# Seven modulation blocks of layer 0: from the tensor engine's products to sums on three other engines

## The chip, the core and the metric

The kernel runs on one core of a Trainium2 chip. The metric is the device time of one execution in microseconds (us), as the median of several runs. The engines are called as the profile calls them: PE (TensorE matmul), PEld (its weight load), DVE (VectorE), ACT (ScalarE), POOL (GpSimd) and SP (SyncE, whose queue issues the DMA transfers). Each engine takes its instructions strictly in the order in which they stand in its queue; an instruction whose inputs are not there holds up everything behind it.

## What is computed

The reference is a stack of three transformer layers on 512 tokens of width 1024, with 256 context tokens. What matters here is the start of layer 0, where every gain and shift comes from two condition vectors (the latent `c` and the context's `c_ctx`) by one product with a 1024 x 6144 matrix:

```python
silu_c, silu_cc = jax.nn.silu(c), jax.nn.silu(c_ctx)
mod_lat = (silu_c @ w_ada[i] + b_ada[i])[:, None, :]
mod_ctx = silu_cc @ w_ada[i] + b_ada[i]
sh_a, sc_a, g_a, sh_m, sc_m, g_m = jnp.split(mod_lat, 6, axis=-1)      # the same split of mod_ctx
h_lat, h_ctx = x * (1.0 + sc_a) + sh_a, xc * (1.0 + csc_a) + csh_a
y_lat, y_ctx = gqa_mixer(h_lat, h_ctx, w_qkv, q_norm, k_norm, w_o, ...)  # q, k, v = h @ w_qkv; norm; rope; attention
x = layer_norm(alpha * x + g_a * y_lat, ...)                            # then the MLP with sh_m, sc_m, g_m
```

Only `sh_a` and `sc_a` are needed before the projections to q, k and v. The gate `g_a` and the three vectors of the MLP are needed after the attention.

## The kernel before

All activations are kept transposed and split into a high and a low part, so that a float32 product is three products in the fast type (`mm3`, lines 137 to 141: one record each on L139, L140 and L141).

The 6144 columns of the modulation are made in 12 blocks of 512 columns. A block is a Python generator whose steps are issued between pieces of other work (`Flow`, lines 61 to 95: every chain that is open takes one step after each piece). For each block two transfers of 1 MB bring 512 rows each of the block's columns into tiles called `adaw`, three of which exist in this stage (`ada_bufs = 3`, line 418). `ada_steps` (line 199) then makes both conditions' products on PE: eight matmuls in four column groups of the array (L217), a copy of the four partial sums to the single tile `row512` by ACT (L221), four transposes of it on PE (L225), and on DVE one sum over the groups (L227) and the addition of the bias (L229), into the tile `MOD0`.

`ada_pooled` (line 231) makes the same vectors another way. In layer 1 it is used for 12 blocks, the first four of them for both conditions, and in the last layer for 12 blocks with one condition. Its steps, with `both=True`:

- two transfers to two `adaw` tiles (L239);
- eight DVE instructions that multiply the eight tiles of rows by the second condition's numbers and add them up into `row512` (L246 once, then L248 seven times, each reading what the one before wrote), and eight ACT instructions that multiply the same tiles by the first condition's numbers in place (L251), each after the DVE instruction that reads the same tile;
- three POOL additions that fold the eight tiles into one, of 2048, 1024 and 512 columns (L255);
- per condition four transposes on PE (L260), then on DVE the sum over partitions (L262) and the bias (L263).

The stage that the change concerns is `gqa` (line 409), from its line 492 to line 519. It holds the projections: for the column blocks `blk` 2 (keys and values), 0 and 1 (queries), and for the six token tiles, `products` issues 24 matmuls per piece and half, the results go from PSUM to `qn`, `kn` and `V` by ACT and DVE, and key chains (`key_steps`) and rope chains (`q_rope`) run beside them. At every second token tile one of the seven open modulation blocks (4, 5, 8, 9, 6, 7, 10) is added to the flow:

```python
if t % 2 and ada:
    flow.add(ada.pop(0))
```

`flow.finish()` (line 518) issues what is left of all chains before the attention's first step, the transposes of queries on L695. A scheduler orders each engine's queue afterwards by priorities and dependencies, so that what the code issues late can stand somewhat earlier. Block 11 is made in the attention, and blocks 0 to 3 before the projections; these five stay as they are.

Of the kernel before, what the change touches and what calls it, by code (L numbers as in the profile page):

```python
# [16 lines left out]
PSUM = bass.MemoryType.PSUM  # L17
# [6 lines left out]
LAG = 4  # L24


class Bump:
    """tiles laid out by hand in given regions of a bigger tile (views [128, n], in its type)"""
# [32 lines left out]
class Flow:  # L61
    """chains of steps that are issued beside the tensor engine's main work"""
# [16 lines left out]
    def finish(self, gen=None):  # L79
        """until the chain (all of them) has ended, beside work that was laid by; the other chains go half as fast"""  # L80
        n = 0
        while gen in self.gens if gen is not None else self.gens:
            if self.fill:
                self.fill.pop(0)()
            n += 1
            self.step([gen] if gen is not None and n % 2 else None)
# [10 lines left out]
class Base:  # L97
# [45 lines left out]
    def rsqrt(self, out, ms, n, scale):  # L143
        """out = (ms * scale + eps) ** -0.5 on [128, n]; ms is overwritten"""
        nc = self.nc
        nc.vector.tensor_scalar(out=ms, in0=ms, scalar1=scale, scalar2=EPS, op0=ALU.mult, op1=ALU.add)
        nc.gpsimd.tensor_tensor(out=out, in0=ms, in1=self.mhalf[:, :n], op=ALU.pow)

# [1 line left out]
    def setup(self):  # L150
        nc, cp, i = self.nc, self.cp, self.i
# [5 lines left out]
        # the activations' split transposes, time-shared by all phases  # L157
# [5 lines left out]
    def load_cols(self, groups, ps, pool, tag, keep=None):  # L163
        """rows of vectors [n, 128] -> one tile of columns; groups: list of (name, ap [n,128])"""
# [34 lines left out]
    def ada_steps(self, a, b, pool, ps, bias, beside=False, spare=False):  # L199
        """512 columns of the modulation vectors: silu(c) @ w (both conditions at once),  # L200
        four row groups of the array at a time, then summed and turned to one column per 128;
        beside: beside an attention's start, in its tiles and those of the weights; spare: the second half in one of these"""
# [28 lines left out]
    def ada_pooled(self, a, b, pool, ps, bias, both=False):  # L231
        """the same beside a phase that leaves the other engines idle: they weigh and sum the rows of a partition (DVE
        for the second condition, if both are asked for); then the sums are turned, and the partitions summed"""
# [19 lines left out]
        x, y = ts  # L253
# [14 lines left out]
    def gains(self, name, sc, sh, g=None, b=None):  # L268
        """columns G, B with h = xhat * G + B for h = (xhat * g + b) * (1 + sc) + sh"""
# [28 lines left out]
    def tok(self, j, k, t):  # L298
        """part j of the split transposed activations: rows of tile k, token tile t (4, 5: the context)"""
# [3 lines left out]
class GqaNet(Base):  # L303
# [1 line left out]
    def gqa_tables(self, kv, pool):  # L305
        """rope tables with the gains of q (and its 1/8) and k folded in: [128, token tile, 64]"""
# [19 lines left out]
    def head_rs(self, pool, x, n, out):  # L326
        """out [128, n] = rsqrt(mean of squares) of the heads of 64 of x [128, n*64]"""
# [14 lines left out]
    def rope64(self, pool, x, n, w, t):  # L342
        """the rope of x [128, n*64], with gains, in place; the context has gains only"""
# [22 lines left out]
    def modulated(self, pool, ps, x, T, gain, c, u):  # L366
        """T's columns from c: the split transpose of a token tile's rows x, times and plus the gain's columns; half u of
        the channels"""
# [18 lines left out]
    def key_steps(self, pool, ps, kn, K, t):  # L387
        """the keys of a token tile: normed, turned by their positions, transposed twice, split"""
# [18 lines left out]
    def gqa(self):  # L407
        nc, i, tc, flow = self.nc, self.i, self.tc, self.flow
        W = i["gqa_w_qkv"][0]
        with ExitStack() as ph:  # L410
# [6 lines left out]
            with tc.tile_pool(name="q0", bufs=1, reuse_waits="tile") as pool, tc.tile_pool(name="q0ps", bufs=2, reuse_waits="tile", space=PSUM) as ps:  # L417
# [8 lines left out]
                def load(t, u):  # L426
                    # the rows wait where the queries come
# [13 lines left out]
                def gains(u):  # L441
                    """columns G, B of half u of the channels, for both conditions"""
# [50 lines left out]
                ada = [self.ada_steps(0, b, pool, ps, None) for b in (4, 5, 8, 9, 6, 7, 10)]  # L493
# [60 lines left out]
    def out_weights(self, W, u):  # L554
        """256 columns of an output projection's weights, split: steps"""
# [10 lines left out]
    def attend(self, units, pool, pss, psp, stages):  # L566
        """softmax attention in units of 128 queries of one head (two, where there are few keys); the scores
        of a unit run LAG units ahead of the transposes of its weights, and their products with v follow
        by the group of four.  stages: unit -> other work beside it, as (PE, then Activation, then DVE) parts"""
# [7 lines left out]
        with self.tc.manual_schedule():  # L577
            for n in range(N + LAG + 6):
# [12 lines left out]
                if n < N:  # L591
# [5 lines left out]
                    if n == 0:  # L597
                        # brings the table of the exponential beside the first maximum
# [41 lines left out]
    def turn(self, pool, psp, g, xs):  # L640
        """the transposed weights of a unit into the group's [128 keys, key tile, head % 2, head // 2, 128]"""
# [19 lines left out]
class GqaGroup:  # L661
    """128 queries of the four heads that share a key head"""
# [11 lines left out]
    def bias(self, xs, m):  # L674
        """minus the scaled maximum"""
# [62 lines left out]
class Seg:  # L738
    """tokens: the split transposed activations T, the sum R [128, 8, n] (first read from S), the gate's columns g"""
# [5 lines left out]
class MlpNet(GqaNet):  # L745
    def stats(self, halves):
        """mean and rsqrt(var + eps) of rows given as PSUM halves [128, 512]: columns 2 and 3 are the factor and the offset"""
# [11 lines left out]
    def rows_of(self, ps, R, c):  # L759
        """the 128 tokens at column c of R as rows, in two halves"""  # L760
# [8 lines left out]
    def along(self, ps, cols):  # L769
        """[128, k, 256]: the columns (k for each of two token tiles) along every row"""  # L770
# [7 lines left out]
    def norm_steps(self, pool, ps, R, c0, res, hs):  # L778
        """layer norm of 256 tokens at column c0 of R [128, 8, n], then per column tile
        R = xhat * res[0] + res[1] (if res) and the split of xhat * G + B (hs: G, B, hi, lo)"""  # L780
# [32 lines left out]
    def w_out(self, W, ps, segs, after):  # L813
        """R = S + g * (T^T W)^T, the product's columns on partitions; the last four column tiles go by groups of
        256 tokens, each followed by the steps after(its number)"""
# [27 lines left out]
    def mlp(self, i, ps, segs, extra, ready, after, zp, gp):  # L843
        """R += g * (relu(h w1)^2 w2)^T in chunks of 256 hidden columns; the first two and the last two chunks go by
        groups of 256 tokens: ready: the steps that a group waits for, after: as in w_out; zp, gp: room"""
# [38 lines left out]
        def one(x, s, c):  # L884
            # a tile's weights are split a piece ahead
# [25 lines left out]
    def cols1(self, pool, ps):  # L911
        """the vectors of block 1 as columns"""
# [9 lines left out]
    def ln_cols(self, i, w, scale):  # L922
        """the gain and bias columns of norm w of layer i times scale"""
# [57 lines left out]
class MlaHead:  # L981
    """the 512 queries of one head; unit x is token tile x"""
    last = 3
# [49 lines left out]
    def low(self):  # L1033
        # a copy of the high part beside the sum where the partitions differ
# [10 lines left out]
class MlaNet(MlpNet):  # L1045
    def mla(self):
# [3 lines left out]
        with ExitStack() as ph:  # L1050
# [6 lines left out]
            # rows of keys and queries by the parity of the head: its 64 plain dims lie at 64 * parity,  # L1057
            # its 32 rotated ones beside them, and the rest are zero
# [18 lines left out]
    def turned_steps(self, pool, ps, xs, gain, hi, lo):  # L1077
        """two token tiles of rows xs, normed, times the gain, into the split columns hi, lo [128, k, 256]"""
# [19 lines left out]
    def mla_in(self, pool, m, spare):  # L1098
        """spare: room for the low part of the query weights, until the keys come"""
# [47 lines left out]
        # the weights of the rotated dims of all heads' queries  # L1147
# [7 lines left out]
        # the rotated dims of the keys  # L1155
# [44 lines left out]
    def turn32(self, out, x, at):  # L1200
        """out (32 rows from row at) = x [128, 32] transposed, as a product with the identity"""
        self.nc.tensor.matmul(out, lhsT=x, rhs=self.ident, start=True, stop=True, tile_position=(0, at))

    def rope32(self, x, tmp, base):
        """x [128, 4, 32] rotated in place"""
# [149 lines left out]
class PreNet(MlaNet):  # L1355
    def row_bcast(self, ps, pool, cols, name, out):
        """out [128, 1024] = the vector in columns [128, 8] along every row"""
# [1337 lines left out]
```

## Time and profile before

| what | value |
|---|---|
| median of 3 runs | 2687.36 us (2686.46 to 2691.48) |
| span of the profiled execution | 2685.0 us |
| PE busy | 2584.2 us, 96% of the span, 14954 instructions |
| DVE, ACT, POOL busy | 1789.9, 1154.3 and 611.1 us (67%, 43%, 23%) |
| chain that ended last | PE 30%, ACT 1%, DVE 1% of the span |

The page is read from the span downwards: PE is busy in nearly all of it, and the chain that ended last is mostly PE. The share of another engine is an average over very different stages, so the prediction goes to the stage itself, the stretch from about 62 to 158 us.

### The profile page before, as it was taken

What the parts mean: (1) busy time and instruction counts of PE and PEld (TensorE: products, weight loads), DVE (VectorE), ACT (ScalarE), POOL (GpSimd) and SP (SyncE); (2) the same over time, 40 slices, a digit from 0 to 9 for tenths busy, and PEclk for the clock granted to TensorE, in tenths of its full rate; (3) what the DMA queues carried; (4) which work ended last, traced back from release to release, by engine and by line L of the source; (5) the groups of instructions that cost most, each with busy time, mean ns of one, the idle gap of its engine ahead of it and who ended that gap; (6) DMA issues with size and microseconds to landing.
All of it is one profiled execution on the core that took longest, in us unless ns stands there. A gap on an engine that the chain in (4) does not pass through costs nothing. (4 is left out here: it accounts for less than half of the span.)

```text
span 2685.0 us, 37836 instructions
## 1 busy us (share of the span) xinstructions
PE 2584.2 (96%) x14954; PEld 2112.6 (79%) x14954; DVE 1789.9 (67%) x3102; ACT 1154.3 (43%) x2016; POOL 611.1 (23%) x445
## 2 busy tenths in 40 slices
PE   8999999999999999999999899989999999999998
PEld 5666689888888898777787678877678888888887
DVE  4558847887777577788489998576675533534445
ACT  4357835333333235655364344253563223532222
POOL 0224322232222013333133234043140011000000
PEclk9999999999999999999999999999999999999999
DMA  8600221333333112010155454233122233222221
GB/s 313 210 32 1 64 95 34 124 128 124 125 111 102 62 38 69 19 33 17 64 167 173 137 176 157 95 110 115 49 66 100 87 94 139 73 94 94 95 94 63
DMA packets 178643, 264.82 MB, mean 99 GB/s; under 512 B 18019, under 2 KB 116954, under 8 KB 177954
## 3 DMA queue, kind: packets, MB, share of 16 engines
q1 hardware_dynamic: 173010, 257.89, 29.2%
q10 hardware_dynamic: 5456, 4.51, 0.6%
q8 instruction: 118, 1.93, 0.3%
q14 instruction: 59, 0.48, 0.1%
HBM read 256.81 MB, written 5.58 MB: 98 GB/s over the span
## 5 line engine op out<-in xcount | busy, mean ns | idle before, releaser
L129 DVE TENSOR_TENSOR wl<-raw,wh 128x1024 fp32r<-128x1024 f32 (+1 forms) x301 | 442.6, 1483 | 305.7 <-ACT wh L126 303.6
L126 ACT CAST wh<-raw 128x1024 fp32r<-128x1024 f32 (+1 forms) x301 | 306.9, 1035 | 611.8 <-PE mm L140 443.7
L139 PE MATMUL mm<-TL,wh 128*128 128x512 f32 (+2 forms) x1512 | 563.2, 374 | 6.0 <-ACT TL L384 4.5
L140 PE MATMUL mm<-TL,wh 128*128 128x512 f32 (+2 forms) x1512 | 558.8, 370 | 4.0 <-DVE TL L385 3.9
L141 PE MATMUL mm<-TL,wl 128*128 128x512 f32 (+2 forms) x1512 | 557.5, 369 | 0.0
L139 PEld LDWEIGHTS mm<-TL,wh 128*128 128x128 f32 (+1 forms) x1512 | 285.1, 189 | 60.2 <-ACT TL L384 5.4
L140 PEld LDWEIGHTS mm<-TL,wh 128*128 128x128 f32 (+1 forms) x1512 | 285.7, 189 | 54.2 <-DVE TL L385 5.6
L141 PEld LDWEIGHTS mm<-TL,wl 128*128 128x128 f32 (+1 forms) x1512 | 285.3, 189 | 52.3
L139 PE MATMUL mm<-TC,wh 128*128 128x256 f32 (+1 forms) x672 | 224.3, 334 | 12.6 <-ACT low L864 12.5
L637 POOL TENSOR_SCALAR p<-p,sm 128x768 f32<-128x768 f32 (+1 forms) x160 | 156.2, 979 | 296.1 <-DVE sm L634 195.3
L141 PE MATMUL mm<-TC,wl 128*128 128x256 f32 (+1 forms) x672 | 223.4, 333 | 0.0
L140 PE MATMUL mm<-TC,wh 128*128 128x256 f32 (+1 forms) x672 | 223.4, 333 | 0.0
L255 POOL TENSOR_TENSOR XN<-XN 128x2048 f32<-128x2048 f32 (+2 forms) x36 | 117.9, 3275 | 297.1 <-ACT XN L251 278.5
L139 PE MATMUL mm<-gh,wh 128*128 128x256 f32 (+1 forms) x544 | 179.6, 330 | 0.0
L140 PE MATMUL mm<-gl,wh 128*128 128x256 f32 (+1 forms) x544 | 178.6, 328 | 0.0
L141 PE MATMUL mm<-gh,wl 128*128 128x256 f32 (+1 forms) x544 | 178.0, 328 | 0.0
L255 POOL TENSOR_TENSOR low<-low 128x2048 f32<-128x2048 f32 (+2 forms) x36 | 111.5, 3097 | 178.4 <-ACT low L251 176.5
L139 PEld LDWEIGHTS mm<-TC,wh 128*128 128x128 f32 x672 | 127.5, 190 | 28.1 <-ACT low L864 13.8
L600 DVE TENSOR_REDUCE sm<-s 128x1 f32<-128x768 f32 (+1 forms) x144 | 132.6, 921 | 22.5 <-PE s L1010 11.4
L140 PEld LDWEIGHTS mm<-TC,wh 128*128 128x128 f32 x672 | 127.8, 190 | 14.1
L141 PEld LDWEIGHTS mm<-TC,wl 128*128 128x128 f32 x672 | 127.7, 190 | 13.1
L657 PE MATMUL pt<-ident,p 128*128 128x128 f32 x768 | 116.1, 281 | 17.7 <-ACT pT L658 7.8
(614 smaller groups left out, 4981.9 us busy)
## 6 DMA issues: line engine op xcount, KB each, us to landing
raw<-in_mlp_w_dram SPq DMA_DIRECT2D x64, 1024.0 KB
raw<-in_w_in_dram SPq DMA_DIRECT2D x26, 1024.0 KB
XN<-in_w_ada_dram SPq DMA_DIRECT2D x24, 1024.0 KB
low<-in_ada_w_dram SPq DMA_DIRECT2D x24, 1024.0 KB
raw<-in_ffn_w_in_dram SPq DMA_DIRECT2D x22, 1024.0 KB
adaw<-in_w_ada_dram SPq DMA_DIRECT2D x21, 1024.0 KB
raw<-in_ffn_w_out_dram SPq DMA_DIRECT2D x11, 1024.0 KB
raw<-in_gqa_w_qkv_dram SPq DMA_DIRECT2D x6, 1024.0 KB
```

The costliest lines, as they stand in the source:

```text
L126: nc.scalar.copy(h, v)
L129: nc.vector.tensor_tensor(l, v, h, op=ALU.subtract)
L139: nc.tensor.matmul(out, lhsT=ah, rhs=bh, start=start, stop=False)
L140: nc.tensor.matmul(out, lhsT=ah, rhs=bl, start=False, stop=False)
L141: nc.tensor.matmul(out, lhsT=al, rhs=bh, start=False, stop=stop)
L255: nc.gpsimd.tensor_tensor(u, u, v, op=ALU.add)
L600: nc.vector.tensor_reduce(out=m[:, 0, :len(xs)], in_=s[:, :g.nk * len(xs)] .rearrange("p (k n) -> p k n", k=len(xs)), axis=AX.X, op=ALU.max)
L637: nc.gpsimd.tensor_scalar(out=g.p[xs][:, c], in0=g.p[xs][:, c], scalar1=m[:, 2, k:k + 1], scalar2=1.0, op0=ALU.mult, op1=ALU.mult)
L657: nc.tensor.transpose(tp[:, 128 * (x - lo):128 * (x - lo) + 128], p[:, 128 * x:128 * x + 128], self.ident)
```

## The change

One line of `gqa` differs: the seven blocks beside the projections are made by `ada_pooled` for both conditions instead of `ada_steps`. (The diff also empties comment lines, which changes no instruction and no line number.)

```diff
-                ada = [self.ada_steps(0, b, pool, ps, None) for b in (4, 5, 8, 9, 6, 7, 10)]
+                ada = [self.ada_pooled(0, b, pool, ps, self.bada[0], True) for b in (4, 5, 8, 9, 6, 7, 10)]
```

`ada_pooled` takes four steps after its transfers where `ada_steps` takes two. How the queues stand around it is shown at three places.

PE, end of the projections. `acc` is the last product of a token tile with the query weights, `tq` the first transposed queries of the attention, `mm` the transposes of a modulation block. Before:

```order
L139 MATMUL acc_1234<-wh_1051,TC0_77 128x512
L140 MATMUL acc_1234<-wl_1052,TC0_77 128x512
L141 MATMUL acc_1234<-wh_1051,TC1_78 128x512
L695 MATMUL tq_1275<-ident_67,qn0_89 128x128 x2
L713 MATMUL s_1286<-K0_86,q0_1278 128x512
```

And now:

```order
L139 MATMUL acc_1346<-wh_1131,TC0_77 128x512
L140 MATMUL acc_1346<-wl_1132,TC0_77 128x512
L141 MATMUL acc_1346<-wh_1131,TC1_78 128x512
L260 MATMUL mm_1216<-ident_67,adaw_1154 128x128 x4
L260 MATMUL mm_1223<-ident_67,row512_72 128x128 x4
L260 MATMUL mm_1305<-ident_67,adaw_1244 128x128 x4
L260 MATMUL mm_1312<-ident_67,row512_72 128x128 x4
L695 MATMUL tq_1387<-ident_67,qn0_89 128x128 x2
```

The transposes of the sixth and the seventh block have come between the last product and the attention's first transposes. Before, the last block's transposes stood 60 matmuls ahead of that place.

DVE, the same stretch. `row512` is the one tile in which the second condition's sum is built; `adaw_1026` and `adaw_1028` are the two tiles of the fifth block, `adaw_1154` and `adaw_1156` those of the sixth. Before, the last two blocks' sums (L227) and biases (L229) stood here directly ahead of the attention's first instruction, L703:

```order
L347 TENSOR_TENSOR qn5_94<-qn5_94,ropeg_215 128x512
L146 TENSOR_SCALAR hms_1070<-hms_1070 128x8
L227 TENSOR_REDUCE MOD0_80<-mm_1115 128x8
L229 TENSOR_TENSOR MOD0_80<-MOD0_80,cols_b_145 128x8
L227 TENSOR_REDUCE MOD0_80<-mm_1188 128x8
L229 TENSOR_TENSOR MOD0_80<-MOD0_80,cols_b_145 128x8
L703 TENSOR_TENSOR q0_1278<-tq_1275,q0_1278 64x256
```

And now, from the fifth block's weighing to the first reduction of the sixth:

```order
L248 SCALAR_TENSOR_TENSOR row512_72<-adaw_1028,silu_79,row512_72 128x512 x4
L262 TENSOR_REDUCE MOD0_80<-mm_1099 128x4
L262 TENSOR_REDUCE MOD0_80<-mm_1106 128x4
L263 TENSOR_TENSOR MOD0_80<-MOD0_80,cols_b_145 128x4
L246 TENSOR_SCALAR row512_72<-adaw_1154,silu_79 128x512
L263 TENSOR_TENSOR MOD0_80<-MOD0_80,cols_b_145 128x4
L248 SCALAR_TENSOR_TENSOR row512_72<-adaw_1154,silu_79,row512_72 128x512 x3
L248 SCALAR_TENSOR_TENSOR row512_72<-adaw_1156,silu_79,row512_72 128x512 x4
L262 TENSOR_REDUCE MOD0_80<-mm_1216 128x4
```

The weighing of each block stands behind the reductions of the block before it, which read what PE transposed of that block.

POOL, the third and the fourth block. `krs` and `RS` are the reciprocal roots of the key and query norms, the only POOL work of this stage before:

```order
L147 TENSOR_TENSOR RS_95<-hms_971,mhalf_73 128x8
L255 TENSOR_TENSOR adaw_770<-adaw_770,adaw_772 128x2048
L255 TENSOR_TENSOR adaw_770<-adaw_770 128x1024
L147 TENSOR_TENSOR RS_95<-hms_1022,mhalf_73 128x8
L255 TENSOR_TENSOR adaw_770<-adaw_770 128x512
L147 TENSOR_TENSOR RS_95<-hms_1082,mhalf_73 128x8
L147 TENSOR_TENSOR RS_95<-hms_1150,mhalf_73 128x8
L255 TENSOR_TENSOR adaw_915<-adaw_915,adaw_917 128x2048
```

Twenty-one additions have been put into that queue, with `krs` and `RS` jobs between and ahead of those of the first four blocks.

## Rows read from the trace of the kernel before

**Rows 1.** The page: span, and the busiest engine's time, share and count.

```profile
span 2685.0 us, 37836 instructions
...
PE 2584.2 (96%) x14954; PEld 2112.6 (79%) x14954; DVE 1789.9 (67%) x3102; ACT 1154.3 (43%) x2016; POOL 611.1 (23%) x445
```

**Rows 2.** Engines by stretch of the projections; the first row names the columns.

```profile
core 0: us, PE busy (x) PEld busy (x) DVE busy (x) ACT busy (x) POOL busy (x), PEclk, DMA share, GB/s
60.00:80.00 20.00, 19.78 (x110) 12.92 (x109) 15.72 (x45) 12.52 (x30) 4.41 (x4) 1.00 0.77 264
...
120.00:140.00 20.00, 20.00 (x105) 13.67 (x103) 3.06 (x7) 3.73 (x7) 1.64 (x1) 1.00 0.47 155
```

**Rows 3.** PE groups, 57 to 158 us: count, busy us, mean ns, idle before.

```profile
L217 PE MATMUL mm<-adaw,silu 128*32 128x512 f32 x112 | 13.7, 599 | 0.0
L225 PE MATMUL mm<-ident,row 128*128 128x128 f32 x28 | 4.2, 274 | 0.0
```

**Rows 4.** PE in order of time: start, us, line, tiles; end of the projections.

```profile
157.34 0.40 PE L141 MATMUL acc<-wh,TC 128*128 128x512 f32 x1
157.58 0.38 PE L695 MATMUL tq<-ident,qn 128*128 128x128 f32 x2
```

**Rows 5.** DVE in order of time: a pooled block of layer 1, almost alone.

```profile
351.15 0.49 DVE L246 TENSOR_SCALAR row<-XN,silu 128x512 f32<-128x512 f32 x1
351.67 3.11 DVE L248 SCALAR_TENSOR_TENSOR row<-XN,silu,row 128x512 f32<-128x512 f32 x4
...
357.84 2.31 DVE L248 SCALAR_TENSOR_TENSOR row<-XN,silu,row 128x512 f32<-128x512 f32 x3
```

**Rows 6.** DVE, ACT and POOL: a pooled block of layer 1 among other work.

```profile
555.39 0.48 DVE L246 TENSOR_SCALAR row<-XN,silu 128x512 f32<-128x512 f32 x1
...
565.01 1.51 ACT L251 ACTIVATE XN<-XN,silu 128x512 f32<-128x512 f32 x2 [0.27 <-DVE row L248]
...
566.65 9.66 POOL L255 TENSOR_TENSOR XN<-XN 128x2048 f32<-128x2048 f32 x3 [24.97 <-ACT XN L251]
```

**Rows 7.** PE and DVE: the transposes and reductions that end such a block.

```profile
548.99 0.60 PE L260 MATMUL mm<-ident,XN 128*128 128x128 f32 x4
...
550.15 1.28 DVE L262 TENSOR_REDUCE MOD<-mm 128x4 f32<-128x512 f32 x2
...
551.81 0.15 DVE L263 TENSOR_TENSOR MOD<-MOD,cols_b 128x4 f32<-128x4 f32 x1
```

**Rows 8.** DVE where the change puts the first weighing.

```profile
64.22 0.42 DVE L359 TENSOR_TENSOR kn<-kn,ropet 128x256 f32<-128x256 f32 x1
```

**Rows 9.** DVE: rope work of one query tile, 512 columns an instruction.

```profile
92.06 0.76 DVE L356 TENSOR_TENSOR rtmp<-qn,ropet 128x256 f32<-128x256 f32 x2 [2.46 <-ACT qn L513]
92.74 0.68 DVE L385 TENSOR_TENSOR K<-mm,K 128x512 fp32r<-128x512 f32 x1
...
93.94 0.68 DVE L359 TENSOR_TENSOR qn<-qn,ropet 128x512 f32<-128x512 f32 x1
```

**Rows 10.** POOL groups, 1511.8 to 1520.6 us: the three additions at their shortest.

```profile
L255 POOL TENSOR_TENSOR low<-low 128x2048 f32<-128x2048 f32 x1 | 4.7, 4671 | 22.0 <-ACT low L251 22.0
L255 POOL TENSOR_TENSOR low<-low 128x1024 f32<-128x1024 f32 x1 | 2.4, 2416 | 0.1
L255 POOL TENSOR_TENSOR low<-low 128x512 f32<-128x512 f32 x1 | 1.3, 1302 | 0.1
```

**Rows 11.** DVE: the split of weights, without and beside POOL's additions.

```profile
74.06 1.22 DVE L129 TENSOR_TENSOR wl<-raw,wh 128x1024 fp32r<-128x1024 f32 x1
...
567.78 4.57 DVE L129 TENSOR_TENSOR wl<-raw,wh 128x1024 fp32r<-128x1024 f32 x1 [2.02 <-ACT wh L126]
```

**Rows 12.** POOL: roots for keys and for queries.

```profile
70.25 1.01 POOL L147 TENSOR_TENSOR krs<-hms,mhalf 128x4 f32<-128x4 f32 x1 [3.78 <-DVE hms L146]
...
86.14 2.06 POOL L147 TENSOR_TENSOR RS<-hms,mhalf 128x8 f32<-128x8 f32 x1 [4.97 <-DVE hms L146]
```

**Rows 13.** PE after waits early in the program, and a stretch's clock.

```profile
12.53 1.08 PE L225 MATMUL mm<-ident,row 128*128 128x128 f32 x4 [0.44 <-ACT row L221]
...
24.00:27.00 3.00, 3.00 (x8) 2.33 (x8) 2.02 (x4) 0.98 (x3) 0.00 (x0) 0.50 1.04 386
```

## The prediction

> **What bounds the kernel now.** I read the page first: PE is busy in 96% of a span of 2685.0 us [rows 1], so what leaves PE could shorten the program, and what makes PE wait lengthens it. An average says nothing of one stage, so the next view is the engines by stretch of the projections [rows 2]. The reader is to see two things. PE is full there (19.78 and 20.00 us of 20) at full clock. DVE is well loaded at the start (15.72 of 20) and nearly idle towards the end (3.06), ACT likewise, and POOL does next to nothing. There is room on three engines, but room is not yet cover: a chain through all three has a length of its own. So I read last the views in order of time of the pooled blocks of layer 1, to see how long one such block takes from its first weighing to its last bias [rows 5 to 7], and laid seven of them behind one another.
>
> **What leaves PE.** The seven blocks' matmuls are 112 records of 13.7 us; their 28 transposes are 4.2 us [rows 3]. The change drops the former and doubles the latter: 13.7 - 4.2 = 9.5 us less PE work. ACT's seven copies of about 0.6 us go too; ACT waits for PE there, so I cost that at nothing.
>
> **What the change builds: one chain in place of seven.** Before, PE made a block's sums at once and only two short links followed. Now a block goes DVE and ACT, POOL, PE, DVE, and blocks cannot overlap, for three reasons in the code and the queues: the second condition's sum has one tile, `row512`, so the next block's first weighing must wait until PE has transposed this one's; ACT multiplies in place, so it trails DVE tile by tile: its wait ended with DVE's `row` [rows 6]; and POOL's first addition needs all eight of ACT's products. On PE the `row512` transposes stand behind those of POOL's sum, so they wait for POOL as well. The transposes of the last two blocks stand ahead of the attention's first instruction, so the attention cannot begin before the seventh block has gone through.
>
> The price of each link, from rows:
>
> *Weighing.* Alone: 0.52 us from the first instruction to the second, then 7 x 0.78 (3.11 for four, 2.31 for three), so 6.0 us [rows 5]; ACT's last product ends about 0.7 us later and POOL starts 0.13 after that (565.01 + 1.51, then 566.65) [rows 6]: 6.8 us. Among other work it took 566.65 - 555.39 = 11.26 us. In the new DVE queue the first four blocks have 8, 9, 9 and 8 other instructions between first and last weighing: rope and split instructions of 512 columns at 0.6 to 0.68 us [rows 9], key ones of 256 columns at 0.33 to 0.42 [rows 8]. I count 2.7 + 2.9 + 4.0 + 3.9 = 13.5 us. The last three blocks have none. Sum: 7 x 6.8 + 13.5 = 61.1 us.
>
> *Additions.* 9.66 us with DVE at work [rows 6], 4.67 + 2.42 + 1.30 plus two gaps of 0.1 = 8.6 us at their shortest [rows 10]. Blocks 1 to 4 have split, key and rope work beside them, blocks 5 to 7 none, since DVE then waits for PE: 4 x 9.66 + 3 x 8.6 = 64.4 us. That DVE work and the additions hold each other up is to be seen: a split of 1.22 us took 4.57 while POOL added [rows 11]. The Trainium skill, "SBUF — State Buffer", section "Who interferes with whom", states it as a rule: a DVE instruction with two SBUF inputs and a GpSimd instruction that reads SBUF exclude each other for the whole instruction. By it blocks 5 to 7 take the short price; if it did not hold, the short price would stand for all seven and the sum would be 4 us less.
>
> *Roots in POOL's queue.* Two `krs` jobs of 1.01 us lie between additions, one `RS` job of 2.06 us lies between and one ahead of them [rows 12]: 6.1 us, all on the chain.
>
> *Transposes and reductions.* From the first transpose (548.99) to the end of the two reductions (550.15 + 1.28 = 551.43) and one bias of 0.15: 2.6 us until the next block's first weighing [rows 7]; six times, and after the seventh 1.0 us of transposes: 16.6 us.
>
> *Splits ahead of the reductions.* After blocks 1 and 3 two splits of 1.22 us stand in DVE's queue ahead of, or among, the reductions and slip past POOL's end: about 4 us.
>
> *Clock.* A PE that has waited transposes more slowly: four took 1.08 us after waits early in the program [rows 13] against 0.60 [rows 7], and three microseconds after another wait ran at a granted clock of 0.50 (1.2 GHz) [rows 13]. Seven blocks of eight transposes could pay 7 x 0.96 = 6.7 us; the trace has no such place in this stage, so the bounds are 0 and 6.7, and I take the middle, 3.4.
>
> *Transfers* I cost at nothing. A block's second tile comes free when the block before has done its first addition; its 1 MB at 264 GB/s [rows 2] is 4.0 us, and it is first read after the other two additions, the transposes and four weighings, some 9 us later. Behind those transfers on SP stand the query weights for the last column block, which the splits need only 40 us later.
>
> **The sum.** The first weighing stands in DVE's queue where L359 starts at 64.2 us [rows 8]. 64.2 + 61.1 + 64.4 + 6.1 + 16.6 + 4 + 3.4 = 219.8 us. The attention's first transposes started at 157.6 [rows 4]. Does PE arrive in time at each block's transposes? Between them stand 24 to 72 matmuls of 0.24 us [rows 4], 6 to 17 us, against 19 to 25 us for a block: PE waits every time, and the 9.5 us saved turn into waiting. So the attention starts 62 us later. Behind it the queues are as before, so nothing is given back: 2685.0 + 62 = 2747 us of span. The median stands 2.4 us above the span, so **2749 us**.
>
> **Rivals.**
> - *The cover holds* (faster). If the chain were done when PE comes to it, PE's saving would be seen: 2687.4 - 9.5 = 2678 us. That needs seven blocks in 157.6 - 9.5 - 64.2 = 84 us, 12 us each; POOL's additions alone are 8.6 and the weighing 6.8. For it speaks only that three engines have room [rows 2]. 3%.
> - *The bare chain* (slower by half). If DVE's other work, the roots and the splits slip into gaps of the chain instead of lengthening it, and the additions are short: 64.2 + 7 x 6.8 + 7 x 8.6 + 16.6 = 188.6, 31 us later: 2718 us. For it speaks that dependent weighings leave small holes on DVE; against it, that both engines take their queues in order. 13%.
> - *Everything at the crowded price.* If additions and DVE's two-input instructions exclude each other wherever they meet, the weighings included, each block pays 11.26 + 9.66, with transposes at the low clock: 64.2 + 7 x 20.9 + 6 x 3.6 + 2 + 10 = 244, 86 us later: 2774 us. Against it, the last three blocks have no other work to meet. 9%. The rule named above would lead there only if weighings and additions overlapped, which the chain forbids.
> - *No change.* Only if the scheduler's place for the last transposes did not bind; the queue shows that it does. 2%.
>
> **How the numbers follow.** The forecast has 73%, with a range of its own of 2736 to 2762: 4 us of clock and 4 of splits either way, and some 6 for the count of DVE work between the weighings. For 8 in 10 the range reaches towards the bare chain and the crowded price: 2724 to 2768. A measurement of this kernel can tell about 0.2%, 5 us. Faster by more than that 3%, within it 2%, slower 95%.
>
> **What would show it.** In the changed kernel's trace: the attention's L695 near 220 us instead of 157.6; PE idle before L260 with POOL as what ended it, some 6 to 18 us at each of seven blocks; POOL's seven sets of additions 19 us apart at the end, 22 to 25 at first; PE's clock at half after those waits; and every later stage of the same length as before. I am wrong if a set of additions begins before the transposes of the block before, if the sets are less than 15 us apart, or if the time after the attention's start changes by more than a few us.

## The result, and the profile after

| | before | after |
|---|---|---|
| median | 2687.55 us (2686.46 to 2691.48, 4 runs) | 2751.0 us (2749.31 to 2753.05, 4 runs) |
| span of the profiled execution | 2685.0 us | 2748.7 us |
| attention's first transposes (L695) | 157.58 us | 216.36 us |

The ratio is 1.0231, with a 95% interval of 1.0219 to 1.0243: the change makes the kernel 63 us slower. 2749 us had been forecast, from 2724 to 2768. The page of the changed kernel, beside [rows 1]:

```profile
PE 2592.7 (94%) x14870; PEld 2128.6 (77%) x14870; DVE 1856.3 (68%) x3172; ACT 1187.4 (43%) x2065; POOL 669.0 (24%) x466
```

PE has 84 records fewer and yet 8.5 us more busy time. The stretch of the projections says why; its columns are those of [rows 2], with PEclk, the granted clock, eighth:

```profile
60.00:80.00 20.00, 15.00 (x70) 11.39 (x68) 19.05 (x35) 13.74 (x28) 9.63 (x5) 1.00 0.25 85
...
120.00:140.00 20.00, 11.71 (x44) 9.40 (x43) 16.01 (x18) 7.11 (x10) 12.35 (x5) 0.74 0.40 132
...
180.00:200.00 20.00, 8.59 (x31) 6.50 (x29) 7.72 (x17) 6.15 (x9) 8.10 (x3) 0.67 0.30 103
200.00:220.00 20.00, 4.00 (x15) 3.42 (x16) 7.76 (x14) 7.79 (x11) 8.10 (x3) 0.50 0.00 0
```

PE was full or nearly so in every such stretch; now it works 15.00, 11.71, 8.59 and 4.00 us of 20. DVE is nearly full at first (19.05 of 20), though part of that is time in which its instructions are held up, as is shown further down. From 120 us on no other engine is full either, which is what one chain over several engines looks like. The waits from 60 to 225 us (total, times, longest) name its links:

```profile
PE mm L260 <- POOL adaw L255: 56.5, 7, 15.8
DVE MOD L262 <- PE mm L260: 49.0, 10, 12.0
POOL adaw L255 <- ACT adaw L251: 41.4, 7, 11.3
```

PE waits for POOL at all seven blocks, DVE for PE, and POOL for ACT, in a circle. In order of time, first PE, then POOL; the number in brackets is the idle time before a row and what ended it:

```profile
106.78 1.12 PE L260 MATMUL mm<-ident,adaw 128*128 128x128 f32 x4 [5.82 <-POOL adaw L255]
...
157.90 1.12 PE L260 MATMUL mm<-ident,adaw 128*128 128x128 f32 x4 [4.42 <-POOL adaw L255]
...
214.60 1.11 PE L260 MATMUL mm<-ident,adaw 128*128 128x128 f32 x4 [15.78 <-POOL adaw L255]
215.51 1.06 PE L260 MATMUL mm<-ident,row 128*128 128x128 f32 x4
216.36 0.63 PE L695 MATMUL tq<-ident,qn 128*128 128x128 f32 x2
...
221.25 3.25 PE L217 MATMUL st<-raw,silu 128*32 128x512 f32 x16
224.43 0.44 PE L695 MATMUL tq<-ident,qn 128*128 128x128 f32 x2
```

```profile
149.47 8.37 POOL L255 TENSOR_TENSOR adaw<-adaw 128x2048 f32<-128x2048 f32 x3 [0.53 <-ACT adaw L251]
168.90 8.35 POOL L255 TENSOR_TENSOR adaw<-adaw 128x2048 f32<-128x2048 f32 x3 [11.06 <-ACT adaw L251]
188.55 8.26 POOL L255 TENSOR_TENSOR adaw<-adaw 128x2048 f32<-128x2048 f32 x3 [11.30 <-ACT adaw L251]
206.29 8.26 POOL L255 TENSOR_TENSOR adaw<-adaw 128x2048 f32<-128x2048 f32 x3 [9.49 <-ACT adaw L251]
```

The attention's L695 comes at 216.36 instead of 157.58 [rows 4], 58.8 us later. Its second pair, at 224.43, stood at 162.96 before: 61.5 us later, since the first step of the attention runs slowly behind the last waits, whose stretch has a granted clock of 0.50 (the 16 matmuls of block 11 took 3.25 us, before 1.92). From there the distance changes by little more than 2 us: layer 1's first additions start at 422.45 us, before at 361.10, a difference of 61.35. The span ends 63.7 us later.

### The profile page after: what moved, and what is told of

It reads as the page before. It is cut to its first block, busy times and chain, and to the rows that moved or that the text cites. A ratio compares the mean times of both kernels' runs of the same rounds, so it can differ in the third digit from the quotient of the medians.

```text
span 2748.7 us, 37826 instructions
## 1 busy us (share of the span) xinstructions
PE 2592.7 (94%) x14870; PEld 2128.6 (77%) x14870; DVE 1856.3 (68%) x3172; ACT 1187.4 (43%) x2065; POOL 669.0 (24%) x466
## 3 DMA queue, kind: packets, MB, share of 16 engines
q8 instruction: 117, 1.92, 0.3%
## 5 line engine op out<-in xcount | busy, mean ns | idle before, releaser
L129 DVE TENSOR_TENSOR wl<-raw,wh 128x1024 fp32r<-128x1024 f32 (+1 forms) x301 | 451.4, 1513 | 305.0 <-ACT wh L126 303.0
```

What stands on the lines that cost most here:

```text
L129: nc.vector.tensor_tensor(l, v, h, op=ALU.subtract)
```

## The experiments

The executions of the kernel before spread over some 5 us, and what a stage gains is blurred behind it: the runs without additions (e2) and before stand 11.0 us apart at layer 1's first additions and 6.1 us at the end. So the experiments are compared by the attention's first transposes as well, 157.6 before and 216.4 after. The runs e1 to e9 were timed once each, e11 five times, e10 and e12 eleven times.

### e2, e3 and e7: are the additions the link that decides?

e2 leaves POOL's three additions out of layer 0, e3 makes them on DVE, e7 leaves out the first alone (the comments name the run):

```diff
-        for u, v in ((x, y), (x[:, :2], x[:, 2:]), (x[:, :1], x[:, 1:2])):
+        for u, v in ((x, y), (x[:, :2], x[:, 2:]), (x[:, :1], x[:, 1:2])) if a else ():   # e2
-            nc.gpsimd.tensor_tensor(u, u, v, op=ALU.add)
+            (nc.gpsimd if a else nc.vector).tensor_tensor(u, u, v, op=ALU.add)             # e3
+        for u, v in ((x, y), (x[:, :2], x[:, 2:]), (x[:, :1], x[:, 1:2]))[a == 0:]:        # e7
```

> The changed kernel without the 21 additions on POOL in layer 0 (this leaves the first condition's sum incomplete: only one of eight tiles of rows is transposed). My theory: the additions are 60 of the about 150 us of the chain and the part that no other engine's work hides; without them a block is 6.8 + 2.6 us plus 13.5 us of other DVE work in all, about 144 us at the end, and PE, at work until 148, is the bound again: attention at 148 to 156, time 2678 to 2688 us. Rival, that the weighings on DVE and ACT between PE's transposes make the chain as long as it is: more than 2715 us.

> The changed kernel with the 21 additions of layer 0 on DVE in place of POOL; all else the same. My theory: the chain stays serial and each block gets shorter by the difference of the additions' prices. A DVE split of 1024 columns is 1.22 us, so 2048, 1024 and 512 columns should take about 2.3 + 1.2 + 0.65 = 4.2 us against 8.3 to 9.7, and no exclusion with POOL is left, nor do the roots stand in the chain's queue: 64 + 7 x (6.8 + 4.2) + 13.5 + 16.6 + 3 + 2 = 176 us for the attention's start, time 2703 to 2714 us. Rival, that DVE's load rather than the chain's length matters (DVE has 15.7 of 20 us at work at first): no gain or a loss, 2748 us or more.

> In layer 0 GpSimd's addition of 2048 columns is left out (rows 512 to 1023 are then missing from the first condition's sums); those of 1024 and 512 stay. Theory (the additions lie on the chain with their whole length): seven times 4.7 us less, 33 us: 2714 to 2722 us, the attention at 180 to 188 us, sets of additions 14 to 16 us apart at the end instead of 19.5. Rival (it is the handing over between engines that costs, not the length of the additions): less than half of that comes back, 2735 us or more.

Measured: e2 2680.8 us (attention at 146.5), e3 2710.9 (179.0), e7 2706.6 (175.3). e2 and e3 came in the times expected, though e2's attention began 1.5 us before its range and e3's 3 us later than reckoned. In e2 PE waits for none of the blocks:

```profile
146.51 0.38 PE L695 MATMUL tq<-ident,qn 128*128 128x128 f32 x2
```

and what PE saves becomes visible, 157.58 - 146.51 = 11.1 us, 1.6 us a block. But the same kernel shows how thin the cover is even without additions. By stretch (DVE is the third of the five busy times):

```profile
60.00:80.00 20.00, 18.81 (x94) 14.97 (x93) 18.97 (x48) 14.34 (x30) 3.40 (x3) 1.00 0.57 205
80.00:100.00 20.00, 20.00 (x101) 16.28 (x100) 19.48 (x44) 17.42 (x34) 3.65 (x3) 1.00 0.56 194
100.00:120.00 20.00, 20.00 (x94) 16.35 (x93) 19.55 (x38) 13.79 (x20) 7.87 (x3) 1.00 0.72 252
120.00:140.00 20.00, 20.00 (x97) 15.93 (x96) 18.80 (x38) 14.02 (x22) 4.47 (x3) 1.00 0.55 185
```

DVE is busy 76.8 of 80 us, before 39.1: the weighings and their reductions fill it. That leaves e3 little room. In its DVE queue the first addition takes half as long as on POOL (4.63 us for the second block of the changed kernel):

```profile
72.44 2.28 DVE L255 TENSOR_TENSOR adaw<-adaw 128x2048 f32<-128x2048 f32 x1
```

but at the end the blocks queue up and PE, the first busy time in e3's row for this stretch, mostly stands still, at a granted clock of 0.63:

```profile
140.00:160.00 20.00, 4.74 (x21) 3.49 (x19) 16.09 (x21) 10.37 (x15) 0.65 (x1) 0.63 0.38 127
```

e7 gained more than its theory, 44 us instead of 33. The edit did two things: without the first addition POOL also no longer waits for ACT's products of the second tile. Its first set starts at 67.35 us instead of 72.59, and the last two stand 11.9 us apart instead of 17.7:

```profile
153.72 4.06 POOL L255 TENSOR_TENSOR adaw<-adaw 128x1024 f32<-128x1024 f32 x2 [4.79 <-ACT adaw L251]
165.64 4.28 POOL L255 TENSOR_TENSOR adaw<-adaw 128x1024 f32<-128x1024 f32 x2 [7.86 <-ACT adaw L251]
```

(These are POOL's rows of e7 in order of time.) So the direction is shown, and the size is not that of the addition alone.

### e1 and e8: is it the single sum tile, or the weight tiles?

e1 gives the second condition's sum two tiles in turn (the second in the room of a table no longer needed). e8 adds to this that the second half of each block's weights goes to the two tiles of the projections' weights, so that five tiles serve the blocks.

```diff
...
-                ada = [self.ada_pooled(0, b, pool, ps, self.bada[0], True) for b in (4, 5, 8, 9, 6, 7, 10)]
+                row2 = [self.row512, pool.tile([P, 512], F32, name="ropeb", tag="ropeb", bufs=1)]
+                ada = [self.ada_pooled(0, b, pool, ps, self.bada[0], True, row2[n % 2]) for n, b in enumerate((4, 5, 8, 9, 6, 7, 10))]
...
+            t = self.wp.tile([P, 2048], F32, name="raw", tag="raw", bufs=2).rearrange("p (k n) -> p k n", k=4) if spare and half \   # e8 alone
+                else pool.tile([P, 4, 512], F32, name="adaw", tag="adaw", bufs=self.ada_bufs)
```

> The changed kernel with two tiles for the second condition's sum, used in turn (the second lies where the rope base was), and nothing else. My theory, one serial chain held together by that one tile: a block's weighing no longer waits for the transposes of the block before, so what is left between two blocks is the supply of the three weight tiles (first addition 4.6 us, a transfer of about 4, four weighings of 3.1 us and ACT's last product 0.7) and POOL's 8.3 to 9.7 us: 13 to 15 us a block in place of 19 to 25. Attention's first transposes at 168 to 178 us in place of 216.4, time 2700 to 2712 us. Rival, that POOL's additions and the other engines' load set the pace and the tile does not matter: 2745 to 2752 us, attention near 216.

> Two tiles for the second condition's sum, and the second half of each block's weights in one of the two tiles of the projections' weights, so that five tiles serve the blocks instead of three. Theory (after the sum tile, the supply of weight tiles holds the blocks in a row: a tile comes free only when a set's first addition is done): sets 10 to 13 us apart, 2700 to 2718 us. Rival (additions and weighings, now side by side, exclude each other, and the queue of VectorE holds the reductions ahead of the weighings): 16 us apart as with two sum tiles alone, 2735 to 2750 us.

Measured: e1 2743.7 us (attention at 207.9), e8 2741.1 (211.2). My theory of the sum tile missed: of 58.8 us it explains 8.5, and more weight tiles give nothing (two of the five are shared with the projections' weights; what that sharing costs was not tried apart). DVE in e1 (a weighing alone takes 0.78 us [rows 5]):

```profile
164.41 6.54 DVE L249 SCALAR_TENSOR_TENSOR ropeb<-adaw,silu,ropeb 128x512 f32<-128x512 f32 x3
175.71 0.69 DVE L263 TENSOR_REDUCE MOD<-mm 128x4 f32<-128x512 f32 x1 [4.75 <-PE mm L261]
...
177.37 3.11 DVE L249 SCALAR_TENSOR_TENSOR ropeb<-adaw,silu,ropeb 128x512 f32<-128x512 f32 x4
...
181.56 9.44 DVE L249 SCALAR_TENSOR_TENSOR row<-adaw,silu,row 128x512 f32<-128x512 f32 x3
```

Two things take the tile's place. Weighings that now fall beside additions are held up: three of them took 6.54 and 9.44 us, not 2.3. And in DVE's queue the reductions of the block before (L263), which wait for PE and so for POOL, stand in front of the second half of the weighing. With e8 it is the same: its sixth set starts at 182.59 us after 11.96 us of waiting for ACT's products, which trail those weighings.

### e5 and e9: without the weighing

e5 makes only the first condition (no weighing on DVE, no sum tile; the context's vectors of the seven blocks are zero); e9 does this with five weight tiles.

```diff
-                ada = [self.ada_pooled(0, b, pool, ps, self.bada[0], True) for b in (4, 5, 8, 9, 6, 7, 10)]
+                nc.vector.memset(self.MOD[0][:, 16:44, 1], 0.0)
+                ada = [self.ada_pooled(0, b, pool, ps, self.bada[0]) for b in (4, 5, 8, 9, 6, 7, 10)]
```

> The changed kernel with only the first condition in the seven blocks (the context's vectors of these blocks are left out and set to zero): no weighing on DVE, no use of the one sum tile, four transposes a block in place of eight; ACT's products and POOL's additions stay. My theory: without the sum tile the blocks overlap, ACT weighs the next block while POOL adds this one, and POOL's pace of 8.3 to 9.7 us plus 6 us of roots in all fits into PE's 84 us; PE is rid of 13.7 us and gains no transposes: 2674 to 2690 us, attention at 144 to 160. Rival, that POOL's additions alone are too slow for this place: attention later than 165 and more than 2697 us.

> Only the first condition is made (the context's vectors of the seven blocks are set to zero), no sum tile is used, and five weight tiles serve the blocks instead of three. With three the time was 2715.5 us, and the last sets stood 12.6 us apart. Theory (the wait for a weight tile, which the first addition frees, 4.7 us + about 4.5 of transfer + 3 of ScalarE's products = 12.2 us, set that distance): sets 8.6 to 9.7 us apart, PE hardly waits, 2674 to 2692 us. Rival (the additions and the order of the queues alone set it): still 12 us apart or more, 2705 to 2720 us.

Measured: e5 2715.5 us (attention at 181.9), e9 2714.2 (177.5). Both theories missed and the times are the rivals'; of e9's sets only the last pair stands closer than its rival's 12 us. In e9 POOL is busy 58.66 of 70 us, as the row for 90 to 160 us shows (the last of the five busy times):

```profile
90.00:160.00 70.00, 51.73 (x205) 41.13 (x205) 49.75 (x57) 38.98 (x65) 58.66 (x25) 0.85 0.48 151
```

ACT is held up by other work in its queue, in order of time before the fourth block's additions. The squares `hsq` wait for DVE's reduction L333, and that one stands behind two rope products (L357), which took 6.96 us beside the third block's additions, not 0.76 [rows 9]. First DVE, then ACT:

```profile
101.40 6.96 DVE L357 TENSOR_TENSOR rtmp<-qn,ropet 128x256 f32<-128x256 f32 x2 [3.15 <-ACT qn L515]
```

```profile
109.65 0.63 ACT L331 ACTIVATE hsq<-qn 128x512 f32<-128x512 f32 x1 [5.69 <-DVE hms L333]
...
112.02 2.55 ACT L252 ACTIVATE raw<-raw,silu 128x512 f32<-128x512 f32 x4
```

and POOL starts when the last of these products is there:

```profile
114.65 4.78 POOL L256 TENSOR_TENSOR adaw<-adaw,raw 128x2048 f32<-128x2048 f32 x1 [0.43 <-ACT raw L252]
```

So POOL's additions delay, by way of DVE and ACT, the products that its own next set needs: here ACT lost 5.69 us in front of the fourth block's. POOL's additions and roots alone are 76.2 us of work from 60 to 180 us, against the 84 us of cover that the forecast had counted; that leaves little to make such losses good. Only the last two sets, at 145.65 and 154.05 us, stood 8.4 us apart.

### e4 and e6: the first four blocks, the last three

```diff
+                ada = [self.ada_pooled(0, b, pool, ps, self.bada[0], True) for b in (4, 5, 8, 9)]          # e4
+                ada += [self.ada_steps(0, b, pool, ps, None) for b in (6, 7, 10)]                         # e6: the other way round
```

> The first four blocks go the new way, the last three stay with TensorE's products. Theory (every block is a chain that PE waits for, wherever it stands): PE waited 7.2, 5.8 and 8.3 us at the first three blocks of the changed kernel and some 6 at the fourth, 27 us; less 4 x 1.4 us of PE work saved, plus about 1 us of low clock: 2708 to 2716 us, the attention's first transposes at 178 to 186 us. Rival (only the last blocks, which have nothing behind them to cover the chain, cost): the waits at the first blocks would be made good by later slack, and the time is 2680 to 2690 us.

> The mirror of the run with the first four blocks: those stay with TensorE's products, the last three go the new way, one sum tile. Theory (a chain of 19.5 us per block where VectorE has nothing else to do): the first of them starts its weighing near 106 us, three periods end near 166 us, the attention starts at 165 to 170 us instead of 157.6, of which PE's saving of 3 us is already taken: 2694 to 2702 us. With four blocks at 38 us (9.5 each) these three would cost some 9 us, 3 each. Rival (a block costs the same wherever it stands, 61.5 / 7 = 8.8 us): 2712 to 2716 us.

Measured: e4 2722.2 us (attention at 188.1), e6 2704.8 (171.8). The blocks cost at both places, 7.6 us each in e4 and 4.7 in e6. The two delays, 30.5 and 14.2 us, are together 14.1 less than the 58.8 of all seven: in e6 each of the three waits is 4.2 us, where the changed kernel's last two are 10.24 and 15.78. Both attentions are later than I reckoned (178 to 186, 165 to 170). In e4 the step that failed is the clock, which I had priced at about 1 us. In e6 I had counted the attention from the end of the chain, with no term for the clock; its last transposes start at 161.29 us, and 8.6 us of the projections' products still stand behind them. In e4 PE waits no more after the fourth block and yet starts slowly:

```profile
159.36 1.12 PE L260 MATMUL mm<-ident,adaw 128*128 128x128 f32 x4 [4.39 <-POOL adaw L255]
...
162.11 1.94 PE L217 MATMUL mm<-adaw,silu 128*32 128x512 f32 x8
...
165.27 1.07 PE L217 MATMUL mm<-adaw,silu 128*32 128x512 f32 x8
```

The same eight matmuls take 1.94 us after the wait and 1.07 three microseconds later. What low clock costs in all is the rest when the waits at the transposes are taken from the delay of the attention, and PE's saving of 1.6 us a block is put back:

| kernel | attention later | waits at the transposes | saving put back | rest |
|---|---|---|---|---|
| after | 58.8 | 56.5 | 11.1 | 13.4 |
| e4 | 30.5 | 25.3 | 6.4 | 11.6 |
| e6 | 14.2 | 12.6 | 4.8 | 6.4 |
| e10 (below) | 3.6 | 5.8 | 4.8 | 2.6 |

PE's other waits before the attention differ by 0.4 us at most, so the rest is work done more slowly. Where PE is the bound again after its waits, each microsecond of waiting cost about another half.

### e10, e11 and e12: a version that is hidden

Four blocks stay on PE, early and close together; the last three are spread, with a sum tile of their own. In e10 they go by ACT, DVE and POOL with three further pieces of cover; in e11 DVE alone weighs and sums both conditions; e12 has e11's places with all seven on PE.

```diff
+                ada = {(2, 1): 4, (2, 3): 5, (2, 5): 8, (0, 0): 9, (0, 1): 6, (0, 4): 7, (1, 1): 10}   # (blk, t): block
+                ada = {x: self.ada_steps(0, b, pool, ps, None) if n < 4 else self.ada_pooled(0, b, pool, ps, self.bada[0], True, rowb)
+                       for n, (x, b) in enumerate(ada.items())}                                          # e12: n < 7
+            for k in range(8):                                                                           # e11: all on DVE
+                for cond, out in ((1, row), (0, x[:, 0, :])):
+                    w, s = ts[k // 4][:, k % 4, :], self.S[:, 0, k, cond:cond + 1]
...
+                        nc.vector.scalar_tensor_tensor(out=out, in0=w, scalar=s, in1=out, op0=ALU.mult, op1=ALU.add)
+                if k % 2:
+                    yield
```

> Four blocks by TensorE's products, early and close together; the last three by sums on ScalarE, VectorE and GpSimd, 6 pieces of the projections apart, with a sum tile of their own and three more pieces between the additions and the transposes. Theory (with the chain shorter than the distance of its place on PE, only PE's saving is left, 7.1 us / 7 = 1.0 us a block as the run without additions showed): 3 us faster than before, 2683 to 2687 us, no wait of PE at the transposes. Rival (splits that GpSimd's additions hold up, or the last block, which has only 6 pieces, make PE wait, and its clock falls): 2690 to 2700 us.

> As the run before, but VectorE alone weighs and sums both conditions of the last three blocks (16 instructions of 0.75 us, 12 us a block), so that neither ScalarE nor GpSimd takes part and nothing excludes anything. Theory (VectorE had 3 of 20 us of work at that place, so the chain is covered): 3 us faster than before, 2683 to 2687 us. Rival (the last block's 12 us stand in front of the splits or of the reductions, and PE waits): 2688 to 2696 us.

> A control for the kernel in which VectorE alone makes the last three blocks: its seven blocks stand at the same places among the projections, but all are made by TensorE's products. Theory (the gain there is PE's work of three blocks, 4.8 us at the attention's start, and the places give nothing): within 0.1% of the kernel before, the attention's first transposes at 157 to 158 us. Rival (the earlier, denser places of the first blocks are what gains): 0.2 to 0.4% faster than before, the attention at 153 to 155 us.

| kernel | median | before, timed beside it | ratio, 95% interval | attention |
|---|---|---|---|---|
| e10 | 2690.95 us | 2690.79 us | 1.0001 [0.9992, 1.0010] | 161.2 |
| e11 | 2681.04 us | 2690.79 us | 0.9963 [0.9951, 0.9976] | 152.8 |
| e12 | 2689.88 us | 2688.77 us | 0.9998 [0.9989, 1.0007] | 157.3 |

e11 is faster than the kernel before by 0.24 to 0.49%, more than its theory had (2683 to 2687 us). e10's rival came true, by one wait and the clock after it, on PE in order of time:

```profile
137.29 1.12 PE L262 MATMUL mm<-ident,adaw 128*128 128x128 f32 x4 [5.79 <-POOL adaw L256]
```

e11, in which a block goes through DVE alone before its transposes, has no such wait: the transposes run at full clock, and the attention starts 4.76 us earlier, 1.6 us for each of three blocks, as e2 has it. PE in order of time, the last block's first transposes and the attention:

```profile
149.16 0.60 PE L275 MATMUL mm<-ident,adaw 128*128 128x128 f32 x4
...
152.82 0.38 PE L713 MATMUL tq<-ident,qn 128*128 128x128 f32 x2
```

The row of e11 for 120 to 140 us, with PE full at full clock:

```profile
120.00:140.00 20.00, 20.00 (x92) 16.31 (x91) 19.09 (x34) 1.76 (x3) 2.07 (x1) 1.00 0.40 137
```

DVE's 19.09 of 20 us shows that a fourth block would hardly fit; that was not tried. The control e12 starts its attention at 157.29 and is no faster than before, so the places give nothing. The timed gain of e11 (6.5 to 13.2 us by the interval) is larger than the 4.8 us that the trace accounts for; what the rest is stays open.

## Why the prediction was right, step by step

The chain as it was, in us; a set is the three additions with the roots between them:

| block | first weighing | set starts | set ends |
|---|---|---|---|
| 1 | 63.61 | 72.59 | 83.31 |
| 2 | 86.46 | 96.33 | 106.73 |
| 3 | 109.46 | 120.80 | 133.07 |
| 4 | 137.92 | 149.47 | 157.84 |
| 5 | 160.58 | 168.90 | 177.25 |
| 6 | 179.99 | 188.55 | 196.81 |
| 7 | 199.47 | 206.29 | 214.55 |

No first weighing stands before the set end of the block before it: seven blocks behind one another, as forecast. The terms, summed over the columns:

| term | forecast | measured |
|---|---|---|
| first weighing | 64.2 | 63.6 |
| weighings, to the set's start | 61.1 | 65.4 |
| sets with the roots | 64.4 + 6.1 | 66.6 |
| transposes, reductions, splits, clock | 16.6 + 4 + 3.4 | 20.7 |
| attention's first transposes | 219.8 | 216.4 |

**The weighings** were 4 us too short in the forecast. The last three blocks have next to nothing between them on DVE and still took 8.3, 8.6 and 6.8 us, where I had 6.8 each: in two of them POOL's set began 2.3 and 2.6 us after DVE's last weighing (166.59 and 185.98), not 0.8 as in [rows 6], since ACT's products trailed further.

**The additions** were priced at the longer of two rows for four blocks; the first addition took 4.63 us in the second block, and at the end whole sets came out at 8.3 us, a little below the shortest in [rows 10]. Of the roots 4.5 us lay between additions. The `RS` jobs ahead of the third and the fourth set were not on the chain, as the forecast had it for one of them: both ended before ACT's last product was there. That additions and DVE work hold each other up is to be seen again, beside [rows 11], in DVE's order of time:

```profile
72.94 4.58 DVE L146 TENSOR_SCALAR hms<-hms 128x4 f32<-128x4 f32 x1
...
121.99 4.86 DVE L129 TENSOR_TENSOR wl<-raw,wh 128x1024 fp32r<-128x1024 f32 x1 [0.70 <-ACT wh L126]
```

In groups from 60 to 216 us:

```profile
L146 DVE TENSOR_SCALAR hms<-hms 128x8 f32<-128x8 f32 (+1 forms) x11 | 15.0, 1363 | 0.0
L129 DVE TENSOR_TENSOR wl<-raw,wh 128x1024 fp32r<-128x1024 f32 x6 | 14.0, 2360 | 1.5 <-ACT wh L126 1.5
```

In e2, without additions, the same two groups take 1.8 and 7.1 us. So some 20 us of DVE's busy time in the changed kernel is time held up.

**PE's waits** were 4.4 to 15.8 us, against 6 to 18 forecast (three of the seven, 5.82, 4.42 and 4.74, are shorter than the forecast's least); the sets stand 17.7 to 19.7 us apart at the end (19 forecast) and 23.7, 24.5 and 28.7 at first (22 to 25 forecast; the 28.7 holds four splits and an `RS` root). Later stages kept their length, but for the attention's first step, where low clock added 2.7 us that no term had. Transfers cost nothing: no engine's wait of this stage ends with a DMA by the profile.

**PE's saving** was taken from busy sums, 13.7 - 4.2 = 9.5 us [rows 3]; e2 and e11 show 1.6 us a block, 11.1 us. It did turn into waiting.

**The clock** was the worst sized. I priced the transposes alone, 3.4 us. PE's busy time up to the second pair of L695 is 105.39 us (60 to 224.43) against 100.58 before (60 to 162.96), with 11.1 us less to do: low clock cost about 16 us. Here most of it lay in time in which PE would have waited anyway, so the sum did not miss it. In e4 and e6, where PE is the bound again, the same error made my forecasts too low.

**The reason that I gave first was not enough.** I wrote that blocks cannot overlap because of the sum tile, the products in place, and the additions' need of all of them. e1 takes the first away and gains 8.5 us of 58.8; e5 and e9 take the sum tile and the weighing away, and the attention is still 20 to 24 us late. What the prediction did not see is that the work does not fit: DVE's idle time (39.1 us busy of the 80 from 60 to 140 us before) is filled by the weighings and reductions (76.8 of 80 us in e2), and POOL's additions, which hold up DVE's instructions and are held up by them, would have to run beside that. How much of the delay is the additions' length and how much the holding up is not separated, since e2 and e3 change both. From the fourth block on the length alone counts: DVE stood idle for 10.3 to 12.0 us before each block's reductions, so none of its work fell beside the additions. So the forecast of the time rested on the length of the chain and held; the reason why there is only one chain was more than the code's three dependencies, and the rival in which the cover holds was further away than its 12 us a block said.

**That the time came within 2 us is partly luck.** The chain ended 3.4 us earlier than forecast, with weighings 4.3 us longer, sets 3.9 and the remaining terms 3.3 us shorter; behind the attention's start, where the forecast had nothing, 4.9 us came on top, 2.7 of them in its first step.

## What to carry to other kernels

An engine's idle share is room for work only if the work, counted instruction by instruction, fits together with all that excludes it: add up the busy time of the engines that block each other before moving anything to them. In these runs a chain over several in-order engines was hidden only where it was shorter than the distance to the place where the bound engine reads its result; fewer blocks, on one engine, farther apart (e11) gave what seven on three engines could not. And a wait of PE cost more than its length wherever PE was the bound again behind it (e4, e6, e10).

## What the runs showed of the hardware

- **A small DVE instruction can wait out a whole addition.** L146, a multiply-add of 4 columns, takes 0.17 us alone; begun just behind POOL's first addition it took 4.58, as in the row above, and again 4.61 at 96.37 us. Both times it ended within 0.03 us of that addition (77.52 and 77.49, 100.98 and 100.96). The Trainium skill, "SBUF — State Buffer", section "Who interferes with whom", counts `tensor_scalar` among the instructions that may take the shared port pair, and says that whoever comes first keeps it for the whole instruction. The trace agrees, with as few columns as 4; and with the weighings, which have two SBUF inputs, 6.54 and 9.44 us for three in e1, where 2.3 is their time alone.
- **Low clock outlasts the wait.** Among waits of 4.4 to 15.8 us the granted clock was 0.50 to 0.89 in each stretch of 20 us from 80 to 220 us, and PE's next work took 1.7 to 1.9 times as long: transposes 1.12 us instead of 0.60, 16 matmuls 3.25 instead of 1.92. In e11, where PE never waited for a block, the stretch shown has 1.00.
